# Block inversions with X and XT in the blocks' own tiles, negations on ScalarE, a third result buffer, and v turned one block later

## The chip, the core and the metric

The kernel runs on one core of one Trainium2 chip. The metric is the time of one execution on the device in microseconds (us): the median of three runs before is 1490.18 us (1489.36 to 1492.62). A core has the engines TensorE (PE in the profile, with its weight loads as PEld), VectorE (DVE), ScalarE (ACT), GpSimd (POOL) and SyncE (SP, which here only issues transfers); each runs its own instructions in their order and waits on semaphores for the others. ScalarE and GpSimd issue transfers too.

## The reference, cut to what matters

One layer of a diffusion backbone over 256 context tokens and 1024 latent tokens, so 10 tiles of 128 tokens, with a model width of 1024:

```python
h   = modulated rms_norm of context and latent tokens
p   = h @ w_in                  # q, k, v, z (4 heads of 128), ab, rq, rk, rv, rg
q, k, v = silu(short_conv(q, k, v))     # 5 taps along the tokens
# gated DeltaNet, in chunks of 64 tokens, forward and backward:
A   = tril(kb @ k.T * decay, -1)
sol = solve_triangular(A + I, [v * beta, kb * exp(G)])
S   = gl * S + k_dec.T @ (u - w @ S)    # scan over the chunks
# retention with rotary positions on rq, rk
y   = concat(rms_norm(o_gdn) * silu(z), group_norm(o_ret) * silu(rg))
x   = x + g1 * (y @ w_out)
x   = x + g2 * swiglu(modulated rms_norm(x))
out = rms_norm(x)
```

The change is in the triangular solve (the inverse of `A + I`), in the convolution of v, and in the order of the projections around them.

## The kernel before

The program is written stage by stage, and a scheduler then interleaves the instructions of each engine by its own simulation of the time; so an engine's final order differs from the written one, and a small edit may move many rows. Tiles are taken from pools; a pool that is opened where others were closed takes their room, so its first writer waits for the last readers of what lay there.

Products in full precision are split in a high and a low part: `whi` on ScalarE, `wlo` on VectorE, and three products for each. **Projection columns** come in groups of 256 (`token_major(g, ...)`, its rows are `tm` L371 to L373): one group over the latent tiles is 8 tiles of 24 matmuls, 192 rows. Groups 8 and 9 are z, finished by `fin_gate` on ScalarE; groups 2 to 5 are rk and rq, finished by `fin_rope` on VectorE (L524, L527) and GpSimd (L529), and their result leaves the three `tm` banks of PSUM only by that. **Convolved heads** come from `conv_block` (`b` L605 to L607, 48 to 72 matmuls; taps on VectorE L615; silu on ScalarE L618) into a tile `y`. There are two `y`, one for each of two heads under way.

Around the change the written order is: convolve k, then q; groups 6 and 7; then for batches 0 and 1 (four tiles of tokens each; batch 2 has two) `solve`: for each tile `pre` (`kk` L729, `kq` L734, a broadcast load `gw`, a select on GpSimd, an exponential on ScalarE, and U L748 and `sp` L750 on VectorE), then `invert`; then the four heads of v, each convolved and at once turned by ten transposes (`vT` L871), copied (`vt` L873) and stored; then `pre` of batch 2, `merge(0)`, the load of the rotary table `rope`, `invert(2)`, `merge(1)`, `merge(2)`; then groups 8 and 9, and the scan, with the retention and groups 2 to 5 beside it.

`invert(b)` inverts all 32x32 diagonal blocks of a batch at once, one block a partition. U's blocks are stored to `yd`, loaded again as `yr`, copied or turned into L (L774, L775); X is set to the identity by GpSimd (L771, L772); 31 steps of two VectorE instructions (L781, L783) substitute forward; the turned inverse XT is written to a tile of L's ring (L785); X and XT go to `xd` (L787). X has one buffer and yr one. `merge(b)` then loads the inverses into U and `t64` (L802, L803) and joins blocks to 64 and to 128 by small matmuls on TensorE: products of 32 rows (L822), their negation `xt1` (L825), two more products (L829, L832), copies on ScalarE (L835, L838), and for every eight matrices products of 64 rows (L845), a negation `xt2` (L846), products (L849), a copy (L851). Both negations are on VectorE. U is stored to `sd` (L853), where the scan loads it (`pk`). The pools GM, G2, GI and GU hold the merges' matrices, and are closed behind groups 8 and 9.

Of the kernel before, what the change touches and what calls it, by code (L numbers as in the profile page):

```python
# [8 lines left out]
F32 = mybir.dt.float32  # L9
# [29 lines left out]
def build(nc, tc, ap, dbg=None, stop=None, marks=None):  # L39
# [19 lines left out]
    def close(p):  # L59
        p_close.pop(id(p)).close()  # L60
# [130 lines left out]
    try:  # L191
# [197 lines left out]
        def token_major(g, tiles, finish, store, pl, q=S):  # L389

            w = [tm_weights(g, kh, pl, q) for kh in range(2)]

            for p in range(0, len(tiles), 2):
                pair = [(t, tm_bank(g)) for t in tiles[p:p + 2]]
                for kh in range(2):
                    for t, o in pair:
                        tm_half(o, w[kh], kh, t)
                for t, o in pair:
                    tm_store(g, t, o, finish, store, pl)
# [118 lines left out]

        def fin_rope(t, o, res):
            cos, sin = rope[:, t, 0:64], rope[:, t, 64:128]  # L520
            ra = R1.tile([P, 2, 2, 64], F32, tag="ra", name="ra")
            o4 = o.rearrange("p (h a d) -> p h a d", a=2, d=64)
            r4 = res.rearrange("p (h a d) -> p h a d", a=2, d=64)
            V.tensor_tensor(ra.rearrange("p h a d -> p (h a) d"), o.rearrange("p (g d) -> p g d", d=64),  # L524
                            bc(cos, [P, 4, 64], 1), ALU.mult)
            for a in range(2):
                V.tensor_tensor(r4[:, :, a, :], o4[:, :, 1 - a, :], bc(sin, [P, 2, 64], 1), ALU.mult)  # L527
            for a, op in ((0, ALU.subtract), (1, ALU.add)):
                G.tensor_tensor(r4[:, :, a, :], ra[:, :, a, :], r4[:, :, a, :], op)  # L529
# [88 lines left out]
            S.activation(y[:, a0:], y[:, a0:], AF.Silu)  # L618

        def newy():  # L620
            return CV.tile([P, NTOK], F32, tag="y", name="y", bufs=2)

        a4, b4, kds4, neG4 = (sm[n].rearrange("p (t d h) -> p t d h", d=2, h=4) for n in ("ab", "beta", "kds", "neG"))

# [39 lines left out]
        V.tensor_scalar(sm["g"], sm["neG"], -1.0, None, ALU.mult)  # L664
        V.tensor_scalar(nkf, nkf, EPS, None, ALU.add)

        lnk = log(GS, nkf, TT * H, "ln").rearrange("p (t h) -> p t h", h=H)
        nG4 = sm["nG"].rearrange("p (t d h) -> p t d h", d=2, h=H)
        V.tensor_scalar(lnk, lnk, 0.5, None, ALU.mult)
        Gr = R2.tile([P, TT, 2, H], F32, tag="Gr", name="Gr", bufs=1)  # L670
# [87 lines left out]
        def invert(b):  # L758

            nc_ = len(BATCH[b])  # L760
            nu = nc_ * H
            nb = 4 * nu
            xd = xds[b] = dr.tile([4 * nb, 1024], F32, tag="xd%d" % b, name="xd%d" % b)
            yr = GI.tile([P, 1024], F32, tag="yr", name="yr", bufs=1)
            for k in range(4):
                SY.dma_start(yd[b][:, k].rearrange("u i j -> i u j"),
                             us[b][q32[k]].rearrange("p e c h j -> p (e c h) j")[:, :, q32[k]])
            SY.dma_start(yr[:2 * nb], yd[b].rearrange("u k i j -> (u k) (i j)"))
            L = GI.tile([P, 1024], F32, tag="L", name="L", bufs=2)
            X = GI.tile([P, 1024], F32, tag="X", name="X", bufs=1)  # L770
            G.memset(X, 0.0)  # L771
            G.memset(X[:, 0::33], 1.0)  # L772
            m = lambda t: t[:2 * nb].rearrange("p (i j) -> p i j", j=32)
            S.activation(L[:nb], yr[:nb], AF.Copy)  # L774
            V.tensor_copy(m(L)[nb:], yr[nb:2 * nb].rearrange("p (i j) -> p j i", j=32))  # L775
            for j in range(31):
                n = 31 - j
                tmp = GI.tile([P, 256], F32, tag="tmp", name="tmp", bufs=1)
                t3 = tmp[:2 * nb, :n * (j + 1)].rearrange("p (i c) -> p i c", c=j + 1)
                sh = [2 * nb, n, j + 1]  # L780
                V.tensor_tensor(t3, bc(m(L)[:, j + 1:, j], sh, 2), bc(m(X)[:, j, :j + 1], sh, 1), ALU.mult)  # L781
                xs = m(X)[:, j + 1:, :j + 1]
                V.tensor_tensor(xs, xs, t3, ALU.subtract)  # L783
            XT = GI.tile([P, 1024], F32, tag="L", name="XT", bufs=2)
            V.tensor_copy(m(XT), X[:2 * nb].rearrange("p (i j) -> p j i", j=32))  # L785
            for i, x in enumerate((X[:nb], XT[nb:2 * nb], X[nb:2 * nb], XT[:nb])):
                SY.dma_start(xd[i * nb:(i + 1) * nb], x)  # L787
# [19 lines left out]
        def merge(b):  # L807

            uu, ub, t64 = blocks(b)
            nu = len(BATCH[b]) * H  # L810
            q = q32
            u = [x.rearrange("p c h j -> p (c h) j") for x in ub]
            t = t64


            pairs = [(d, p) + ((2 * p, 2 * p + 1) if d == 0 else (2 * p + 1, 2 * p)) for p in range(2) for d in range(2)]
            three = lambda ps, sl, w: ps[sl].rearrange("p (n j) -> p n j", j=w)
            ps1 = bank_b("m1")
            for n in range(nu):
                for d, p, a, bb in pairs:  # L820
                    ca = (a % 2) * 32
                    T.matmul(ps1[q[bb], n * 32:n * 32 + 32], u[d][q[a], n, q[bb]], t[d][q[a], n, ca:ca + 32],  # L822
                             start=True, stop=True)
            xt1 = GM.tile([P, 16, 32], F32, tag="xt", name="xt1", bufs=1)
            V.tensor_scalar(xt1.rearrange("p n j -> p (n j)")[:, :nu * 32], ps1[:, :nu * 32], -1.0, None, ALU.mult)  # L825
            ps2, ps3 = bank_b("m1"), bank_b("m1")
            for n in range(nu):
                for d, p, a, bb in pairs:
                    T.matmul(ps2[q[a], n * 32:n * 32 + 32], xt1[q[bb], n, :], u[d][q[bb], n, q[bb]],  # L829
                             start=True, stop=True)  # L830
                    if p == d:
                        T.matmul(ps3[q[bb], n * 32:n * 32 + 32], u[d][q[bb], n, q[bb]], xt1[q[bb], n, :],  # L832
                                 start=True, stop=True)
            for d, p, a, bb in pairs:
                S.activation(u[d][q[a], :, q[bb]], three(ps2[:, :nu * 32], q[a], 32), AF.Copy)  # L835
                if p == d:
                    ca = (a % 2) * 32
                    S.activation(t[d][q[bb], :, ca:ca + 32], three(ps3[:, :nu * 32], q[bb], 32), AF.Copy)  # L838
            halves = [(0, slice(0, 64), slice(64, 128)), (1, slice(64, 128), slice(0, 64))]
            for n0 in range(0, nu, 8):  # L840
                ps1, ps2 = bank_b("m2"), bank_b("m2")
                xt2 = GM.tile([P, 8, 64], F32, tag="xt", name="xt2", bufs=1)
                for n in range(8):
                    for d, A, B in halves:
                        T.matmul(ps1[B, n * 64:n * 64 + 64], u[d][A, n0 + n, B], t[d][A, n0 + n, :], start=True, stop=True)  # L845
                V.tensor_scalar(xt2.rearrange("p n j -> p (n j)"), ps1, -1.0, None, ALU.mult)  # L846
                for n in range(8):
                    for d, A, B in halves:
                        T.matmul(ps2[A, n * 64:n * 64 + 64], xt2[B, n, :], u[d][B, n0 + n, B], start=True, stop=True)  # L849
                for d, A, B in halves:  # L850
                    S.activation(u[d][A, n0:n0 + 8, B], three(ps2, A, 64), AF.Copy)  # L851
            for c, t in enumerate(BATCH[b]):
                S.dma_start(sd[t, :, 1:8:6], uu[:, :, c].rearrange("p e h j -> p e (h j)"))  # L853
            checkpoint("mrg%d" % b)

        def solve(b):
            for t in BATCH[b]:
                pre(t)
            checkpoint("pre%d" % b)
            invert(b)  # L860
            checkpoint("inv%d" % b)

        solve(0)
        solve(1)
        for h in range(H):
            y = newy()
            conv_block(8 + h, y, False)
            for t0, n in ((0, 2), (2, 4), (6, 4)):
                ps = bank_a("vT")
                for t in range(t0, t0 + n):  # L870
                    T.transpose(ps[:, (t - t0) * P:(t - t0 + 1) * P], y[:, t * P:(t + 1) * P], ident)  # L871
                vt = CV.tile([P, 4, P], F32, tag="vt", name="vt", bufs=2)
                S.activation(vt[:, :n], ps[:, :n * P].rearrange("p (t j) -> p t j", j=P), AF.Copy)  # L873
                S.dma_start(vd[t0:t0 + n, :, h, :].rearrange("t p j -> p t j"), vt[:, :n])
        close(CV)
        checkpoint("v")
        RP = pool("rp", side="right")
# [13 lines left out]
        merge(2)  # L891


        for g in (8, 9):
            token_major(g, LAT, fin_gate, S, W)
        checkpoint("rgz")
        close(GM)
        close(G2)
# [1 line left out]
        close(GU)  # L900


        SC = pool("sc", bufs=2, side="right")
        PK = pool("pk", side="right")
        dy = dr.tile([LT, P, D], F32, tag="dy", name="dy")
# [247 lines left out]
        close(RT)  # L1153
        close(PK)
        close(SC)
        close(RP)
        close(GS)

# [518 lines left out]
```

## Time and profile before

| what | value |
|---|---|
| median of three runs | 1490.18 us |
| the profiled execution | 1488.32 us |
| its span, first to last instruction | 1486.5 us |
| mean granted TensorE clock | 0.977 |
| busy TensorE / VectorE / ScalarE / GpSimd | 95% / 66% / 42% / 39% of the span |
| TensorE in 360 to 380 us | 11.12 us busy, clock 0.74 |
| TensorE in 520 to 540 us | 20.00 us busy, clock 1.00 |

Sums in the prediction are made against the profiled execution, which was 1.86 us below the median; 1.8 us of it lie outside the span. A row of a view of groups reads: line, engine, operation, what is written and read, how often; busy time and mean of one; the idle time ahead and what ended it. A row of the waits has the sum, how often, and the longest. A row of the timeline has its start, its duration and, in brackets, the wait ahead of it. A row of the windows has the busy time of PE, PEld, DVE, ACT and POOL with the number of instructions, then the granted clock, the share of the DMA engines' time, and GB/s. A row of a list of transfers ends with the time from issue to landing.

### The profile page before, as it was taken

Reading aid. Unit: us, or ns where it says so; the run is one execution under the profiler, and the core shown is the slowest. Engines: PE = TensorE matmul, PEld = TensorE weight load, DVE = VectorE, ACT = ScalarE, POOL = GpSimd, SP = SyncE. Lnnn points to the kernel's source line nnn. Section 1 sums busy time; section 2 is a strip of 40 time slices with the busy share of each in tenths; the row PEclk is TensorE's granted clock in tenths of the full one; section 3 lists DMA queues with packets and bytes.
Section 4 is the critical chain, followed back from the end, with each engine's and each line's share of the span. In section 5 each row is a group of like instructions: output and inputs, shape, how many; then the busy total and the mean of one; then the engine's idle time right before and its main releaser. Section 6 shows DMA issues by size and latency. Waiting matters only on the chain. (4 is left out here: it accounts for less than half of the span.)

```text
span 1486.5 us, 24142 instructions
## 1 busy us (share of the span) xinstructions
PE 1407.3 (95%) x8919; PEld 1207.9 (81%) x8919; DVE 978.0 (66%) x1909; ACT 618.0 (42%) x1342; POOL 579.6 (39%) x493
## 2 busy tenths in 40 slices
PE   7999999996988999899799899999999999999997
PEld 2798888875978999889688688877888888788886
DVE  6568786568666335789777786656555554658577
ACT  5543553866331111346544533323333333444445
POOL 0130010221102344245235588899555553335321
PEclk9999999999889999999899999999999999999999
DMA  9536676478745743996633265765222242685863
GB/s 334 187 105 232 179 235 194 137 221 227 178 130 136 288 165 115 412 367 192 223 124 114 85 210 212 256 236 191 107 107 106 106 145 73 224 293 184 299 220 114
DMA packets 167766, 284.78 MB, mean 192 GB/s; under 512 B 43208, under 2 KB 93592, under 8 KB 163936
## 3 DMA queue, kind: packets, MB, share of 16 engines
q1 hardware_dynamic: 116096, 239.80, 47.6%
q10 hardware_dynamic: 49072, 35.83, 7.8%
q0 software_dynamic: 2480, 7.60, 1.4%
q8 instruction: 70, 1.15, 0.3%
q14 instruction: 48, 0.39, 0.1%
HBM read 201.36 MB, written 81.84 MB: 191 GB/s over the span
## 5 line engine op out<-in xcount | busy, mean ns | idle before, releaser
L371 PE MATMUL tm<-whi,hhi 128*128 128x256 f32 (+1 forms) x704 | 202.7, 293 | 7.5 <-ACT whi L344 3.0
L372 PE MATMUL tm<-wlo,hhi 128*128 128x256 f32 (+1 forms) x704 | 202.8, 290 | 0.7 <-DVE wlo L345 0.7
L373 PE MATMUL tm<-whi,hlo 128*128 128x256 f32 (+1 forms) x704 | 201.4, 290 | 0.0
L371 PEld LDWEIGHTS tm<-whi,hhi 128*128 128x128 f32 x704 | 136.0, 195 | 10.7 <-ACT whi L344 3.2
L372 PEld LDWEIGHTS tm<-wlo,hhi 128*128 128x128 f32 x704 | 137.2, 195 | 2.7 <-DVE wlo L345 1.2
L1366 PE MATMUL ffn<-t,wlo 128*128 128x512 f32 x352 | 137.1, 390 | 1.6 <-DVE wlo L345 1.6
L1364 PE MATMUL ffn<-t,whi 128*128 128x512 f32 x352 | 137.0, 390 | 1.4 <-ACT whi L344 1.4
L373 PEld LDWEIGHTS tm<-whi,hlo 128*128 128x128 f32 x704 | 136.3, 195 | 1.6 <-issue 0.9
L1365 PE MATMUL ffn<-t,whi 128*128 128x512 f32 x352 | 137.0, 389 | 0.0
L344 ACT ACTIVATE whi<-wraw 128x512 fp32r<-128x512 f32 (+2 forms) x98 | 75.2, 771 | 133.1 <-PE ffn L1365 80.2
L344 ACT ACTIVATE whi<-ws 128x512 fp32r<-128x512 f32 x88 | 55.6, 632 | 173.8 <-PE ffn L1365 121.0
L345 DVE TENSOR_TENSOR wlo<-ws,whi 128x512 fp32r<-128x512 f32 x88 | 94.7, 1078 | 48.4 <-ACT whi L344 48.2
L1490 PE MATMUL fo<-whi,ahi 128*128 128x512 f32 x308 | 119.3, 389 | 1.0 <-ACT ahi L344 1.0
L1491 PE MATMUL fo<-wlo,ahi 128*128 128x512 f32 x308 | 119.9, 389 | 0.0
L1492 PE MATMUL fo<-whi,alo 128*128 128x512 f32 x308 | 119.0, 390 | 0.0
L345 DVE TENSOR_TENSOR wlo<-wraw,whi 128x512 fp32r<-128x512 f32 (+2 forms) x92 | 101.5, 1105 | 19.5 <-ACT whi L344 19.2
L1364 PE MATMUL ffn<-b,whi 128*128 128x512 f32 x264 | 103.9, 394 | 5.1 <-ACT whi L344 5.1
L1366 PE MATMUL ffn<-b,wlo 128*128 128x512 f32 x264 | 103.6, 392 | 0.7 <-DVE wlo L345 0.7
L1365 PE MATMUL ffn<-b,whi 128*128 128x512 f32 x264 | 103.4, 392 | 0.0
L615 DVE SCALAR_TENSOR_TENSOR y<-u,cw,y 128x1022 f32<-128x1022 f32 (+3 forms) x80 | 81.9, 1040 | 19.7 <-ACT y L609 19.2
L607 PE MATMUL b<-hhi,wlo 128*128 128x512 f32 (+1 forms) x256 | 94.7, 370 | 0.0
L606 PE MATMUL b<-hlo,whi 128*128 128x512 f32 (+1 forms) x256 | 94.3, 368 | 0.0
(451 smaller groups left out, 3440.1 us busy)
## 6 DMA issues: line engine op xcount, KB each, us to landing
adaw<-ada SPq DMA_DIRECT2D x48, 512.0 KB, 4.4
pk<-sd SPq DMA_DIRECT2D x16, 1536.0 KB, 15.0
wraw<-wfi SPq DMA_DIRECT2D x44, 512.0 KB, 4.2
ar<-ad SPq DMA_DIRECT2D x33, 512.0 KB, 4.2
w<-wfo SPq DMA_DIRECT2D x22, 512.0 KB, 4.3
wd<-tw SPq DMA_DIRECT2D x11, 1024.0 KB, 4.9
ad<-act SPq DMA_DIRECT2D x20, 512.0 KB, 3.1
raw<-wd SPq DMA_DIRECT2D x20, 512.0 KB, 4.7
```

The costliest lines, as they stand in the source:

```text
L344: S.activation(hi, raw, AF.Copy)
L345: e.tensor_tensor(lo, raw, hi.bitcast(F32), ALU.subtract)
L371: T.matmul(o, hhi[:, k, tsl], whi[:, k % 4, :], start=(k == 0), stop=False)
L372: T.matmul(o, hhi[:, k, tsl], wlo[:, k % 4, :], start=False, stop=False)
L373: T.matmul(o, hlo[:, k, tsl], whi[:, k % 4, :], start=False, stop=(k == KT - 1))
L607: T.matmul(o, wlo[:, k, :], hh, start=False, stop=(k == KT - 1))
L1364: T.matmul(o, whi[:, k, :], xhi(xn, slice(0, 4), k), start=(first and k == 0), stop=False, **kw)
L1365: T.matmul(o, whi[:, k, :], xlo(xn, slice(0, 4), k), start=False, stop=False, **kw)
L1366: T.matmul(o, wlo[:, k, :], xhi(xn, slice(0, 4), k), start=False, stop=(k == 3), **kw)
L1490: T.matmul(po[g][i], ahi[:, ts], whi, start=(j == 0 and not kw), stop=False, **kw)
L1491: T.matmul(po[g][i], ahi[:, ts], wlo, start=False, stop=False, **kw)
L1492: T.matmul(po[g][i], alo[:, ts], whi, start=False, stop=(j == FH - 1), **kw)
```

## The change

Four things, in the diff below:

- **invert**: `yr` is gone. The upper rows of the reloaded blocks go straight to X, the lower ones to L, in two loads; L's turned half is copied from X, and then VectorE sets X to the identity. XT is written into L itself. X has two buffers.
- **merge**: both negations are ScalarE copies with a scale of -1.
- **v**: the y tiles are three; head h is turned behind the convolution of head h+1, and head 3 behind group 8, which is written ahead of it now. The copies `vt` hold two transposes each, so there are five stores a head in place of three.
- **room**: the rope stage's temporary `ra` has a pool of its own, RA, opened behind the merges' pools and ahead of the scan's; the temporary of one logarithm moves from the pool GS to R2.

```diff
@@ fin_rope
-            ra = R1.tile([P, 2, 2, 64], F32, tag="ra", name="ra")
+            ra = RA.tile([P, 2, 2, 64], F32, tag="ra", name="ra")
@@ newy
-            return CV.tile([P, NTOK], F32, tag="y", name="y", bufs=2)
+            return CV.tile([P, NTOK], F32, tag="y", name="y", bufs=3)
@@
-        lnk = log(GS, nkf, TT * H, "ln").rearrange("p (t h) -> p t h", h=H)
+        lnk = log(R2, nkf, TT * H, "ln").rearrange("p (t h) -> p t h", h=H)
@@ invert
-            yr = GI.tile([P, 1024], F32, tag="yr", name="yr", bufs=1)
+            L = GI.tile([P, 1024], F32, tag="L", name="L", bufs=2)
+            X = GI.tile([P, 1024], F32, tag="X", name="X", bufs=2)
...
-            SY.dma_start(yr[:2 * nb], yd[b].rearrange("u k i j -> (u k) (i j)"))
-            L = GI.tile([P, 1024], F32, tag="L", name="L", bufs=2)
-            X = GI.tile([P, 1024], F32, tag="X", name="X", bufs=1)
-            G.memset(X, 0.0)
-            G.memset(X[:, 0::33], 1.0)
+            rows = yd[b].rearrange("u k i j -> (u k) (i j)")
+            SY.dma_start(X[nb:2 * nb], rows[nb:])
+            SY.dma_start(L[:nb], rows[:nb])
             m = lambda t: t[:2 * nb].rearrange("p (i j) -> p i j", j=32)
-            S.activation(L[:nb], yr[:nb], AF.Copy)
-            V.tensor_copy(m(L)[nb:], yr[nb:2 * nb].rearrange("p (i j) -> p j i", j=32))
+            V.tensor_copy(m(L)[nb:], X[nb:2 * nb].rearrange("p (i j) -> p j i", j=32))
+            V.memset(X, 0.0)
+            V.memset(X[:, 0::33], 1.0)
...
-            XT = GI.tile([P, 1024], F32, tag="L", name="XT", bufs=2)
+            XT = L
             V.tensor_copy(m(XT), X[:2 * nb].rearrange("p (i j) -> p j i", j=32))
@@ merge
-            V.tensor_scalar(xt1.rearrange("p n j -> p (n j)")[:, :nu * 32], ps1[:, :nu * 32], -1.0, None, ALU.mult)
+            S.activation(xt1.rearrange("p n j -> p (n j)")[:, :nu * 32], ps1[:, :nu * 32], AF.Copy, scale=-1.0)
...
-                V.tensor_scalar(xt2.rearrange("p n j -> p (n j)"), ps1, -1.0, None, ALU.mult)
+                S.activation(xt2.rearrange("p n j -> p (n j)"), ps1, AF.Copy, scale=-1.0)
@@ v
+        def vturn(h, y):
             for t0, n in ((0, 2), (2, 4), (6, 4)):
                 ps = bank_a("vT")
                 for t in range(t0, t0 + n):
                     T.transpose(ps[:, (t - t0) * P:(t - t0 + 1) * P], y[:, t * P:(t + 1) * P], ident)
-                vt = CV.tile([P, 4, P], F32, tag="vt", name="vt", bufs=2)
-                S.activation(vt[:, :n], ps[:, :n * P].rearrange("p (t j) -> p t j", j=P), AF.Copy)
-                S.dma_start(vd[t0:t0 + n, :, h, :].rearrange("t p j -> p t j"), vt[:, :n])
+                for t in range(t0, t0 + n, 2):
+                    vt = CV.tile([P, 2, P], F32, tag="vt", name="vt", bufs=2)
+                    S.activation(vt, ps[:, (t - t0) * P:(t - t0 + 2) * P].rearrange("p (t j) -> p t j", j=P), AF.Copy)
+                    S.dma_start(vd[t:t + 2, :, h, :].rearrange("t p j -> p t j"), vt)
...
+        vys = []
         for h in range(H):
-            y = newy()
-            conv_block(8 + h, y, False)
+            vys.append(newy())
+            conv_block(8 + h, vys[h], False)
+            if h:
+                vturn(h - 1, vys[h - 1])
+        token_major(8, LAT, fin_gate, S, W)
+        vturn(H - 1, vys[H - 1])
         close(CV)
...
-        for g in (8, 9):
-            token_major(g, LAT, fin_gate, S, W)
+        token_major(9, LAT, fin_gate, S, W)
...
+        RA = pool("ra", bufs=2, side="right")
         SC = pool("sc", bufs=2, side="right")
```

The scheduler's order moves with it. TensorE, end of the v part, before (numbers behind a name count tiles; `y_3774` is head 2, `y_3894` head 3, `tm_4895` the first tile of group 8):

```order
L607 MATMUL b2_3956<-hhi_86,wlo_3896 128x512
L734 MATMUL kq_4032<-qc_4030,kc_4023 128x128 x4
L729 MATMUL kk_4065<-kc_4063 128x128 x4
L871 MATMUL vT_3872<-ident_65,y_3774 128x128 x2
L871 MATMUL vT_3878<-ident_65,y_3774 128x128 x4
L871 MATMUL vT_3886<-ident_65,y_3774 128x128 x4
L734 MATMUL kq_4072<-qc_4070,kc_4063 128x128 x4
L871 MATMUL vT_3992<-ident_65,y_3894 128x128 x2
L871 MATMUL vT_3998<-ident_65,y_3894 128x128 x4
L871 MATMUL vT_4006<-ident_65,y_3894 128x128 x4
L371 MATMUL tm_4895<-whi_4883,hhi_86 128x256
```

The same place now, from the last convolution's end to group 8's first row (`y_3754` is head 2):

```order
L607 MATMUL b2_3942<-hhi_86,wlo_3882 128x512
L729 MATMUL kk_4281<-kc_4279 128x128 x2
L734 MATMUL kq_4288<-qc_4286,kc_4279 128x128 x3
L868 MATMUL vT_3978<-ident_65,y_3754 128x128 x2
L868 MATMUL vT_3984<-ident_65,y_3754 128x128 x4
L868 MATMUL vT_3995<-ident_65,y_3754 128x128 x4
L734 MATMUL kq_4288<-qc_4286,kc_4279 128x128
L729 MATMUL kk_4321<-kc_4319 128x128 x4
L371 MATMUL tm_4018<-whi_4006,hhi_86 128x256
```

Head 3's transposes and the last kq have moved behind group 8's 192 rows, ahead of group 9 (`y_3880` is head 3, `tm_4187` group 8's last tile, `tm_5149` group 9's first):

```order
L373 MATMUL tm_4187<-whi_4012,hlo_87 128x256
L868 MATMUL vT_4242<-ident_65,y_3880 128x128 x2
L734 MATMUL kq_4328<-qc_4326,kc_4319 128x128 x4
L868 MATMUL vT_4248<-ident_65,y_3880 128x128 x4
L868 MATMUL vT_4259<-ident_65,y_3880 128x128 x4
L371 MATMUL tm_5149<-whi_5137,hhi_86 128x256
```

TensorE, end of merge 2 before (`U2` and `t64_4742` are batch 2; `tm_5736`, `tm_5813` and those behind are tiles of groups 2 and 3):

```order
L373 MATMUL tm_5736<-whi_5465,hlo_87 128x256
L845 MATMUL m2_4843<-t64_4742,U2_4022 64x64 x15
L371 MATMUL tm_5813<-whi_5801,hhi_86 128x256
L371 MATMUL tm_5814<-whi_5801,hhi_86 128x256
L372 MATMUL tm_5813<-wlo_5802,hhi_86 128x256
...
L373 MATMUL tm_5813<-whi_5807,hlo_87 128x256
L849 MATMUL m2_4844<-U2_4022,xt2_4845 64x64 x16
L948 MATMUL Tr_5372<-pk0_5367 128x128 x4
```

And now, from merge 1's last products to the scan's first transposes (`U1` is batch 1; `tm_5559` is the fourth tile of group 2):

```order
L849 MATMUL m2_4955<-U1_3015,xt2_4956 64x64 x16
L822 MATMUL m1_5006<-t64_4996,U2_4278 32x32 x32
L829 MATMUL m1_5041<-U2_4278,xt1_5039 32x32
L832 MATMUL m1_5042<-xt1_5039,U2_4278 32x32
...
L845 MATMUL m2_5097<-t64_4996,U2_4278 64x64 x16
L849 MATMUL m2_5098<-U2_4278,xt2_5099 64x64 x16
L957 MATMUL Tr_5393<-pk0_5388 128x128 x4
L957 MATMUL Tr_5400<-pk1_5391 128x128 x4
L964 MATMUL up_5407<-vn_5398,pk0_5388 128x128 x4
L371 MATMUL tm_5559<-whi_5480,hhi_86 128x256
```

Before, 276 rows of groups 2 and 3 stood among the merges, the last ones between merge 2's stages; now 72 rows (three tiles of group 2) stand ahead of merge 1's last products, and none from there to behind merge 2 and the scan's first products.

VectorE, where invert 1 ends and invert 2 begins, now (`L_3421` holds XT of batch 1, `X_4627` and `L_4626` are batch 2, `wlo_5481` is group 2's first low part):

```order
L783 TENSOR_TENSOR X_3422<-X_3422,tmp_3522 128x31
L785 COPY L_3421<-X_3422 128x1024
L781 TENSOR_TENSOR tmp_4637<-L_4626,X_4627 64x31
...
L783 TENSOR_TENSOR X_4627<-X_4627,tmp_4652 64x26x6
L345 TENSOR_TENSOR wlo_5481<-wraw_5482,whi_5480 128x4x256
L781 TENSOR_TENSOR tmp_4655<-L_4626,X_4627 64x175
...
L785 COPY L_4626<-X_4627 64x1024
L524 TENSOR_TENSOR ra_5543<-tm_5492,rope_4274 128x256
```

The first low part of group 2 stands behind invert 1 as before, and the first rope stage, which stood in the middle of invert 2, stands behind its end. The copy of batch 2's L, which needs the blocks stored and loaded again, stands ahead of invert 1's last eight steps.

More of the change, by code (lines that the diff above doesn't have):

```diff
@@ L861, in solve @@
             checkpoint("inv%d" % b)
-        solve(0)
-        solve(1)
-        for h in range(H):
-            y = newy()
-            conv_block(8 + h, y, False)
+        def vturn(h, y):
             for t0, n in ((0, 2), (2, 4), (6, 4)):
@@ L871, in build @@
                     T.transpose(ps[:, (t - t0) * P:(t - t0 + 1) * P], y[:, t * P:(t + 1) * P], ident)
-                vt = CV.tile([P, 4, P], F32, tag="vt", name="vt", bufs=2)
-                S.activation(vt[:, :n], ps[:, :n * P].rearrange("p (t j) -> p t j", j=P), AF.Copy)
-                S.dma_start(vd[t0:t0 + n, :, h, :].rearrange("t p j -> p t j"), vt[:, :n])
+                for t in range(t0, t0 + n, 2):
+                    vt = CV.tile([P, 2, P], F32, tag="vt", name="vt", bufs=2)
+                    S.activation(vt, ps[:, (t - t0) * P:(t - t0 + 2) * P].rearrange("p (t j) -> p t j", j=P), AF.Copy)
+                    S.dma_start(vd[t:t + 2, :, h, :].rearrange("t p j -> p t j"), vt)
+        solve(0)
+        solve(1)
+        vys = []
+        for h in range(H):
+            vys.append(newy())
[4 more added lines that the diff above has]
+        vturn(H - 1, vys[H - 1])
         close(CV)
@@ L1155, in build @@
         close(SC)
+        close(RA)
         close(RP)
```

## The prediction

> **What bounds the kernel now.** I read the page first, then the waits of TensorE between 300 and 510 us, then the same stretch cut into windows.
>
> ```profile
> PE 1407.3 (95%) x8919; PEld 1207.9 (81%) x8919; DVE 978.0 (66%) x1909; ACT 618.0 (42%) x1342; POOL 579.6 (39%) x493
> ```
>
> TensorE works 95% of the span, so an edit on another engine pays only where TensorE waits for it or runs at a lowered clock. The edits act where v is convolved and turned (until 373 us) and on groups 8, 9, 2, 3 with the three merges (373 to 500 us). The waits there:
>
> ```profile
> PE vT L871 <- ACT y L618: 11.2, 3, 8.7
> PE kq L734 <- issue: 5.2, 2, 2.6
> PE m L822 <- DMA t<-xd: 4.8, 4, 2.3
> PE tm L371 <- ACT whi L344: 3.0, 1, 3.0
> PE m L829 <- issue: 2.6, 1, 2.6
> ```
>
> So 16.4 us of waits lie in the v part (vT and kq), and 10.4 in the merges. Pauses also cost clock:
>
> ```profile
> 360.00:380.00 20.00, 11.12 (x72) 10.93 (x73) 17.87 (x34) 10.52 (x18) 2.44 (x2) 0.74 0.56 166
> 400.00:420.00 20.00, 16.94 (x397) 16.11 (x398) 16.70 (x41) 5.50 (x10) 0.00 (x0) 0.77 0.43 106
> 440.00:460.00 20.00, 17.90 (x258) 16.78 (x263) 13.97 (x35) 2.55 (x4) 5.10 (x9) 0.83 0.69 181
> ```
>
> The column behind POOL's is the granted clock: 0.74, 0.77 and 0.83 of full. What that does to a row of the projection:
>
> ```profile
> 401.13 0.41 PE L371 MATMUL tm<-whi,hhi 128*128 128x256 f32 x1
> 401.35 0.41 PE L372 MATMUL tm<-wlo,hhi 128*128 128x256 f32 x1
> ...
> 500.84 0.28 PE L373 MATMUL tm<-whi,hlo 128*128 128x256 f32 x1
> 500.96 0.28 PE L371 MATMUL tm<-whi,hhi 128*128 128x256 f32 x1
> ```
>
> Start to start, a row takes 0.12 us at full clock and 0.21 at the lowered one: 0.09 lost for each slow row.
>
> **The v part.** The last head's v is turned right behind its own convolution:
>
> ```profile
> 360.15 1.31 PE L871 MATMUL vT<-ident,y 128*128 128x128 f32 x10 [1.35 <-ACT y L618]
> ...
> 371.08 2.40 PE L871 MATMUL vT<-ident,y 128*128 128x128 f32 x10 [8.73 <-ACT y L618]
> 373.13 0.56 PE L371 MATMUL tm<-whi,hhi 128*128 128x256 f32 x1
> ```
>
> Before 371.08 TensorE has nothing but vT and waits 8.73 us for taps and silu of y; with the third y each head is turned a block later, and head 3 behind all of group 8. Group 8 began at 373.1. Less 16.4 of waits, less 1.1 of slow vT (2.40 against 1.31), less 2.2 for head 3's vT (1.31) and the last kq (about 0.9), which now stand behind group 8, that is 353.4 if nothing new waits. Something will: VectorE, which frees the banks of kk and kq and makes y, was itself busy 17.9 of 20 us in 360 to 380. The order has five places where kq, vT or a convolution needs a bank or a y early. Bounds: none of it, or the old 16.4. The nearest rows are the kq waits of 2.6; I take five of 1 to 2, **7 us** in all, and 1 us of clock. Group 8 begins at **361.4**, 11.7 earlier.
>
> The vt tiles of two transposes cost ACT and its queue two more copies and stores a head. ACT worked 10.5 of 20 us there, so I put this at nothing; uncovered it would be eight copies, under 0.4 us each. The log's temporary costs nothing: same rows, another pool.
>
> **The inversions.** XT in L's place and loads straight into X and L remove the ScalarE copy; the memsets go to VectorE.
>
> ```profile
> DVE xt L825 <- PE m L822: 6.9, 2, 4.9
> DVE xt L846 <- PE m L845: 5.7, 2, 4.2
> DVE tmp L781 <- POOL X L772: 7.6, 2, 5.1
> ```
>
> VectorE stood 12.6 us in merges 0 to 2 before negations, and 7.6 behind GpSimd's memset, which waited for the single X to be stored. Both go. VectorE gains three memsets of 1024. No row shows one there; the bounds are nothing, where VectorE would have waited anyway, and its copy of 1024 elements, 1.13 below; I take 1.0 each, near the copy, plus 0.2 for the diagonal. [...]
>
> The negations go to ScalarE at about 0.6 us, taken from its copies of 512 elements from the same banks (two in 1.19, below). Nothing else needs ScalarE in those stages.
>
> **The path that sets the end of the stretch.** In the new order the rope stage of group 2 (ra) can't start before merge 2's matrices are stored, since ra's pool takes the merges' room. So 72 rows of group 2 fill the three banks, and TensorE then runs the rest of merges 1 and 2 with no projection between. I follow this chain on the clock of the run before.
>
> TensorE: group 8's 192 rows at 0.12 take 23.0 (384.4), vT and kq 2.2 (386.6), 119 rows of group 9 14.3 (400.9), then 76 rows 9.1 with merge 0's two product stages and one of its four 64-row stages. Those I put at 4.5; their busy time in the rows below, 2/5 of three sums and 1/5 of one, is 7.3, an upper bound since rows overlap. At **414.5** it stands at group 2's first row with wlo, the low part of the weights.
>
> ```profile
> L845 PE MATMUL m<-t,U 64*64 64x64 f32 x160 | 6.6, 221 | 0.0
> ...
> L822 PE MATMUL m<-t,U 32*32 32x32 f32 x320 | 5.1, 194 | 4.9 <-DMA t<-xd 4.8
> L829 PE MATMUL m<-U,xt 32*32 32x32 f32 x320 | 5.0, 202 | 2.6 <-issue 2.6
> L832 PE MATMUL m<-xt,U 32*32 32x32 f32 x160 | 4.9, 203 | 0.0
> ```
>
> VectorE: this wlo stands behind invert 1's end, which stands behind invert 2's L copy, its load, the yd store, and the last U of batch 2; the exponential for that U stands on ScalarE behind the 96th row of group 9 (398.1). From there: res 0.4, table load and exponential 1.28 each, U 0.7, store 1.2 and 3.7, loads 1.2 and 4.1, L copy 1.1, memset 1.2, eight rows of invert 1 2.0, XT 1.1, twelve short rows of invert 2 3.1, wlo 1.2: 22.3 more, so 420.4. With 2.5 for queueing (SP also issues merge 0's loads between) **423**. TensorE waits 8.5.
>
> ```profile
> 383.74 1.28 ACT L745 ACTIVATE gw<-gw,nG 128x128 f32<-128x128 f32 x4
> 385.05 1.28 ACT L532 ACT_TABLE_LOAD   x1
> ...
> gw<-grow_d SPq DMA_DIRECT2D x13, 256.0 KB, 4.9
> ...
> yr<-yd SPq DMA_DIRECT2D x2, 512.0 KB, 4.1
> ...
> yd<-U SPq DMA_DIRECT2D x4, 64.0 KB, 3.7
> ```
>
> Head 3's vT closes the convolutions' pool, and rope's load takes that room; on SP's queue gw for that U and half of merge 0's t stand behind it. vT ends at 386.6; with its copy and the wait for its store (about 3) and gw's 4.9 they land near 395 to 397. That is before 398.1 and 400.9, so I add nothing; if it takes 5 more, the chain behind moves with it.
>
> Then invert 2: 62 rows took 21.7 in all (11.1 and 10.6 below), the twelve done 3.1; with a second wlo the end is 19.8 later, 442.8.
>
> ```profile
> L783 DVE TENSOR_TENSOR X<-X,tmp 64x31 f32<-64x31 f32 (+15 forms) x31 | 11.1, 358 | 0.9
> L781 DVE TENSOR_TENSOR tmp<-L,X 64x31 f32<-64x31 f32 (+15 forms) x31 | 10.6, 342 | 3.3 <-POOL X L772 2.5
> ```
>
> From XT to the first full run of merge 2's products took 12.3 before (469.40 to 481.68); in batch 1 21.6 (XT at 428.44, last issue ended 446.65, landing 3.4).
>
> ```profile
> 388.15 1.13 DVE L785 COPY XT<-X 128x1024 f32<-128x1024 f32 x1
> ...
> 428.44 1.06 DVE L785 COPY XT<-X 128x1024 f32<-128x1024 f32 x1
> ...
> 469.40 1.05 DVE L785 COPY XT<-X 64x1024 f32<-64x1024 f32 x1
> ...
> 440.79 5.86 SPq L803 DMA_DIRECT2D t<-xd  x4
> ...
> 481.68 0.70 PE L822 MATMUL m<-t,U 32*32 32x32 f32 x58 [0.73 <-DMA t<-xd]
> ...
> 498.82 1.19 ACT L851 ACTIVATE U<-m 64x512 f32<-64x512 f32 x2 [5.54 <-PE m L849]
> ...
> sd<-U ACTq DMA_DIRECT2D x10, 512.0 KB, 5.6
> ```
>
> I take 12.3, as this is the same batch: merge 2 starts at **455**. Bare, it costs products 0.9 and 1.0, copies 2.2, two 64-row stages of about 1.1, two negations 0.4 and 0.6, some 7.7 with the hand-overs, and 1 for the lowered clock; the copies of U 1.2, the store 0.9 and 5.6, ra and res 0.9: group 2's next row starts at **472**.
>
> By then 456 projection rows are done (192 + 192 + 72). Before, they were these when the scan's first transposes ended, at 500.5:
>
> ```profile
> L371 PE MATMUL tm<-whi,hhi 128*128 128x256 f32 x221 | 66.4, 308 | 4.5 <-ACT whi L344 3.0 <-DVE res L527 1.4
> L372 PE MATMUL tm<-wlo,hhi 128*128 128x256 f32 x220 | 66.2, 303 | 0.3 <-DVE wlo L345 0.3
> L373 PE MATMUL tm<-whi,hlo 128*128 128x256 f32 x219 | 65.9, 303 | 0.0
> ```
>
> That is 660. The transposes are done in the pause now. The other 204 cost 24.5 at 0.12 and 2.4 for some 27 slow rows after the pause: 499. So of the 11.7 us earned, about 10 go back to bare merges, and 1.5 to 2 stay, with 0.5 for the up product that is also done. Behind this point the order on TensorE is nearly the old one.
>
> [...]
>
> **Sum.** The profiled execution took 1488.32 us, 1.86 below the median of the runs (1490.18). 1488.3 less 2.2 is 1486.1; on the median's footing **1488.0**.
>
> **Rivals.** (a) *Shorter stalls, 11 us more gained.* If wlo isn't held by the late U (the exponential passes group 9's results sooner), invert 1 ends by its own work: XT 0 some 9 us earlier than its 388.15, and from XT 0 to XT 1 the old 40.3 less 5.1 for the memset and some 6 for negations and ra: 408 instead of 418. All behind moves by as much: 1477. For it: VectorE sheds 20 us of waits. Against: the chain above, all in a fixed order. (b) *Slower.* Merge 2's transfers take batch 1's 21.6, not 12.3, beside merge 1's stores and the scan's loads: +9.3, net +7: 1495; it decides once merge 2's data come more than 3 us later than 455. For: windows of that stretch show the DMA at 0.43 to 0.69 busy, and the loads now follow closer on the stores. Against: batch 2 is half the size. (c) *The v part isn't shortened*, since VectorE, 17.9 of 20 busy, holds kq and vT as it did: the dates of both chains move 10 to 11 later, and the bare merges remain: 1497. (d) *The merges stay filled*: the forecast's 10 us of giving back don't occur at all; that is (a) by another way.
>
> **Chances.** Forecast 0.47, with a range of its own of 1484 to 1492 (the 7 us of new waits may be 4 or 11, the queueing 0 or 5); (a) and (d) 0.24; (b) 0.21; (c) 0.08. What a measurement can tell from no change here is 0.2%, 3 us. Of the forecast, 0.17 lies below 1487.2 and 0.02 above 1493.2: faster 0.41, same 0.28, slower 0.31. The range runs from (a) to just over (c): **1477 to 1498**.
>
> **What would show it.** Group 8's first row near 361; a wait of TensorE of 6 to 10 us on group 2's wlo near 415; merges 1 and 2 with no projection row inside, and a wait for the loads of t before merge 2; projection rows resuming at 470 to 475. Rival (a) shows as no wait on wlo; (b) as merge 2's first product after 460; (c) as group 8 at 370 or later. Wrong altogether would be a change behind 500 us: I give the scan, the output projection and the FFN nothing.

## The result, and the profile after

The change made the kernel slower. In runs beside one another it took 1497.32 us (1496.62 to 1498.59, 4 runs), the kernel before 1489.77 us (1487.52 to 1492.62, 4 runs): ratio 1.0051, 95% interval 1.0031 to 1.007, so about 7.6 us. The profiled execution took 1496.62 us, 8.3 more than the one before (1488.32). I had forecast 1488.0, a little faster or the same; the time lies inside my range, on its far side. Slow executions are left out of the medians and ratios below: one of e6 (1986.5 us) and two of the kernel before.

The waits of TensorE between 300 and 510 us, after the change, largest first (waiter, what ended the wait, sum, times, longest):

```profile
PE m L845 <- ACT t L838: 5.2, 4, 2.0
PE kS L939 <- DVE S L967: 4.4, 1, 4.4
PE m L822 <- DMA t<-xd: 4.1, 3, 3.4
PE m L829 <- issue: 3.5, 2, 2.5
PE tm L372 <- DVE wlo L345: 3.4, 2, 3.2
PE m L849 <- ACT xt L846: 2.6, 3, 1.2
PE tm L371 <- ACT vt L871: 2.2, 2, 1.1
PE m L829 <- ACT xt L825: 2.0, 1, 2.0
```

The waits of vT on y (11.2) and most of kq's (5.2, now 2.1) are gone. In their place stand waits inside the merges: their products for ScalarE's copies and negations, each between two stages of one merge. The same stretch in windows, after (PE first; behind POOL the granted clock):

```profile
360.00:380.00 20.00, 18.79 (x144) 17.73 (x143) 19.38 (x40) 10.03 (x17) 1.81 (x1) 1.00 0.35 111
400.00:420.00 20.00, 18.31 (x424) 17.22 (x423) 10.01 (x24) 6.77 (x13) 2.39 (x2) 1.00 0.70 155
440.00:460.00 20.00, 11.94 (x405) 10.97 (x405) 11.70 (x33) 5.33 (x10) 0.00 (x0) 0.80 0.66 178
460.00:480.00 20.00, 13.43 (x344) 12.32 (x343) 1.60 (x8) 7.88 (x16) 0.84 (x3) 0.67 0.78 265
```

At 360 to 380 TensorE works 18.79 us instead of 11.12, at full clock. At 440 to 460 it works 11.94 where it had 17.90, and from 460 to 480 it works 13.43 at a clock of 0.67, where before it was:

```profile
460.00:480.00 20.00, 16.99 (x407) 15.87 (x393) 13.20 (x40) 5.79 (x10) 5.85 (x12) 1.00 0.48 127
```

What it does in those 40 us stands in the groups of instructions cut to 440 to 480 us. The projection's three groups before:

```profile
L371 PE MATMUL tm<-whi,hhi 128*128 128x256 f32 x62 | 18.9, 314 | 4.5 <-ACT whi L344 3.0 <-DVE res L527 1.4
L372 PE MATMUL tm<-wlo,hhi 128*128 128x256 f32 x62 | 18.6, 303 | 0.3 <-DVE wlo L345 0.3
L373 PE MATMUL tm<-whi,hlo 128*128 128x256 f32 x61 | 18.2, 301 | 0.0
```

And after the change:

```profile
L372 PE MATMUL tm<-wlo,hhi 128*128 128x256 f32 x11 | 3.9, 357 | 0.0
L373 PE MATMUL tm<-whi,hlo 128*128 128x256 f32 x11 | 3.7, 340 | 0.0
L371 PE MATMUL tm<-whi,hhi 128*128 128x256 f32 x9 | 3.1, 347 | 0.0
```

185 rows against 31: 154 rows fewer, 18.5 us at 0.12 each. That shows that the projection has left the merges, but it isn't the loss, for in the same 40 us the change does 704 of the merges' small matmuls and the kernel before 452: merge 2 ends at 478.3 in the change and at 498.8 before. Counted at the same place of the program, the kernel before has 660 rows done at 500.5, behind the scan's first transposes; the change has 456 done at 483.0, behind these and the first up product (0.8 us). The 204 missing rows are 24.5 us, so there the change is **some 6 us behind** (507.5 against 501.3), although it began group 8 6.7 us ahead. So 13 us went in between; 1.9 of them are head 3's turn and the last kq, which now stand behind group 8. VectorE shows what holds the rows (its waits from 430 to 500 us, after):

```profile
DVE ra L524 <- PE m L849: 25.6, 1, 25.6
```

The first rope stage of group 2 waits 25.6 us for merge 2's last product. The dates of the chain that I had followed, after the change (each row is cut to a short window, so its count is not the whole group):

```profile
366.44 0.38 PE L371 MATMUL tm<-whi,hhi 128*128 128x256 f32 x1
...
446.85 1.38 PE L822 MATMUL m<-t,U 32*32 32x32 f32 x86 [3.42 <-DMA t<-xd]
...
467.60 0.59 PE L822 MATMUL m<-t,U 32*32 32x32 f32 x46
...
478.23 0.58 PE L957 MATMUL Tr<-pk 128*128 128x128 f32 x1
...
483.04 0.36 PE L371 MATMUL tm<-whi,hhi 128*128 128x256 f32 x1
...
493.17 0.58 PE L939 MATMUL kS<-S,pk 128*128 128x128 f32 x1 [4.44 <-DVE S L967]
```

Group 8 starts at 366.4 (before 373.1). Merge 1's products start at 446.9 and merge 2's at 467.6, with nothing to wait for between them but the merge itself; 17 rows stand behind merge 1's first products, and none from 452.4 on. The projection goes on at 483.0.

### The profile page after: what moved, and what is told of

Same layout as the page of the kernel before. It is cut to its first block, busy times and chain, and to the rows that moved or that the text cites. A ratio compares the mean times of both kernels' runs of the same rounds, so it can differ in the third digit from the quotient of the medians.

```text
span 1494.6 us, 24154 instructions
## 1 busy us (share of the span) xinstructions
PE 1402.7 (94%) x8919; PEld 1205.8 (81%) x8919; DVE 971.3 (65%) x1907; ACT 622.4 (42%) x1355; POOL 575.2 (38%) x487
## 4 chain that ended last, share of the span: by engine, by line
PE 50%; DMA 10%; DVE 8%; POOL 6%; ACT 3%; issue 3%; SPq 0%; ACTq 0%; POOLq 0%; DVEq 0%
PE ffn L1376 6%; PE ffn L1374 6%; PE ffn L1375 6%; PE fo L1502 4%; PE fo L1500 4%; PE fo L1501 4%; PE tm L373 3%; PE tm L371 3%; PE tm L372 3%; DMA wd<-tw 2%; PE op L1235 2%; PE op L1234 2%; PE op L1233 2%; DMA t<-xd 1%; POOL ws L1347 1%
## 5 line engine op out<-in xcount | busy, mean ns | idle before, releaser
L371 PE MATMUL tm<-whi,hhi 128*128 128x256 f32 (+1 forms) x704 | 199.3, 288 | 6.0 <-ACT vt L871 2.2
L605 PE MATMUL b<-hhi,whi 128*128 128x512 f32 (+1 forms) x256 | 94.6, 370 | 1.3 <-ACT y L609 1.3
```

Source lines behind the costliest of these rows:

```text
L371: T.matmul(o, hhi[:, k, tsl], whi[:, k % 4, :], start=(k == 0), stop=False)
```

## The experiments

All ran beside the kernel before, which had a median of 1488.9 to 1489.7 us in these runs; e1 to e4 ran on one chip, e5 to e11 on another, so between these the ratios compare better than the medians. Ratios are to it, with 95% intervals; the changed kernel's is 1.0051. The last column counts projection rows between the first and the last matmul of the merges, from the profile of each.

| run | edit | median us | ratio (interval) | rows |
|---|---|---|---|---|
| before | | 1489.77 | 1 | 468 |
| change | | 1497.32 | 1.0051 (1.0031 to 1.007) | 145 |
| e1 | change, ra's pool early | 1484.16 | 0.9965 (0.9952 to 0.9979) | 354 |
| e2 | change, third y only for v | 1506.25 | 1.0112 (1.0098 to 1.0125) | 109 |
| e3 | e1 and e2 together | 1483.06 | 0.9959 (0.9943 to 0.9975) | 352 |
| e4 | change, negations on VectorE | 1502.53 | 1.008 (1.0062 to 1.0098) | 145 |
| e5 | change, head 3 turned inside group 8 | 1502.88 | 1.0105 (1.0083 to 1.0127) | 225 |
| e6 | e1, v turned at once | 1490.35 | 1.0016 (1.0 to 1.0033) | 326 |
| e7 | e1, negations on VectorE | 1485.18 | 0.9976 (0.9959 to 0.9993) | 330 |
| e8 | e1, inversion as before | 1487.66 | 0.999 (0.9976 to 1.0003) | 400 |
| e9 | before, ra's pool late | 1506.44 | 1.012 (1.0093 to 1.0147) | 264 |
| e10 | before, negations on ScalarE | 1482.55 | 0.995 (0.9933 to 0.9968) | 512 |
| e11 | e3, head 3 turned inside group 8 | 1486.78 | 0.9978 (0.9964 to 0.9993) | 403 |

### e1 and e9: the room of ra

e1 takes the changed kernel and opens ra's pool ahead of the merges' pools:

```diff
+        RA = pool("ra", bufs=2, side="right")
         GM = pool("gm", side="right")
...
-        RA = pool("ra", bufs=2, side="right")
         SC = pool("sc", bufs=2, side="right")
```

> Only the pool of the rope temporary is opened ahead of the merges' pools, so it no longer takes their room; all else is the changed kernel. Theory A (the room of ra keeps groups 2 and 3 out of the merges, and the bare merges cost some 19 us against before): projection rows of groups 2 and 3 stand between the stages of merges 1 and 2 again, the q part is unchanged with its wait of about 5 us on qt, and the time falls by 8 to 19 us from 1497, to 1478 to 1489. Rival B (the late chain from the last gw load over invert 1 and invert 2 to the merges' loads sets the pace, whoever owns the room): the waits move to wlo and to the loads of t, and the time stays within 4 us of 1497.

1484.16 us, 13 below the change: theory A held. Rival B fell by the time, though TensorE's wait for merge 1's loads did grow (6.74 us here, 3.42 in the change). In the groups of e1 from 440 to 480 us 148 projection rows are back (31 in the change; this profiled execution took 1489.0 us, 4.8 above e1's median):

```profile
L372 PE MATMUL tm<-wlo,hhi 128*128 128x256 f32 x50 | 15.6, 312 | 0.0
L371 PE MATMUL tm<-whi,hhi 128*128 128x256 f32 x49 | 15.1, 308 | 0.0
L373 PE MATMUL tm<-whi,hlo 128*128 128x256 f32 x49 | 14.9, 304 | 0.0
```

e9 makes the reverse test, that edit alone on the kernel before:

```diff
-            ra = R1.tile([P, 2, 2, 64], F32, tag="ra", name="ra")
+            ra = RA.tile([P, 2, 2, 64], F32, tag="ra", name="ra")
...
+        RA = pool("ra", bufs=2, side="right")
         SC = pool("sc", bufs=2, side="right")
```

> The kernel before with one edit: ra comes from a pool opened behind the merges' pools, as in the change. Theory A (this room alone empties the merges and costs 13 to 19 us net): merges 1 and 2 run with no projection row, and the time is 1502 to 1509. Rival (the loss needs the change's other edits, the late last U and the later turn among them): 1490 to 1498.

1506.44 us: theory A again. This one edit costs 1.2% on the kernel before, 17 to 18 us; the rest of the change together gained 9 to 10. Merge 1's products begin at 455.0 us in e9, as in the kernel before (454.9), and the first row behind the merges comes at 491.7, with 456 rows done. In the change these two dates are 446.9 and 483.0, 8 to 9 us earlier: by these dates, what the other edits gain with bare merges is the earlier start of merge 1. Windows of e9 show the same picture as the change:

```profile
440.00:460.00 20.00, 14.26 (x343) 13.19 (x343) 13.70 (x31) 2.55 (x4) 0.00 (x0) 0.91 0.70 165
460.00:480.00 20.00, 11.92 (x337) 10.47 (x337) 8.14 (x23) 5.78 (x10) 0.00 (x0) 0.55 0.62 162
480.00:500.00 20.00, 14.12 (x135) 13.23 (x135) 4.11 (x15) 4.41 (x10) 4.44 (x9) 0.76 0.98 368
```

TensorE works 11.92 of 20 us at 460 to 480, at a clock of 0.55.

### e2 and e3: the third result buffer

After the change TensorE loses time in the q part too (qt are transposes of q that ScalarE squares and sums): it works 38.80 us of the 45 from 255 to 300, where it had 44.96. Its longest wait there:

```profile
PE qt L686 <- ACT qt L688: 5.4, 1, 5.4
```

With a third y the scheduler had drawn the last q convolution forward; ScalarE then had exponentials, silu, squares and copies mixed, and loaded its tables six times from 265 to 290 us (three times before), 1.28 us each. e2 gives the third buffer to head 2 of v alone, so that k and q have two again:

```diff
-            return CV.tile([P, NTOK], F32, tag="y", name="y", bufs=3)
+            return CV.tile([P, NTOK], F32, tag="y", name="y", bufs=2)
...
-            vys.append(newy())
+            vys.append(CV.tile([P, NTOK], F32, tag="y3", name="y3", bufs=1) if h == 2 else newy())
```

> The third result buffer serves head 2 of v alone; k and q have two again, as before; all else is the changed kernel. Theory A (the third buffer lets the scheduler draw the last q convolutions forward, ScalarE then alternates between exponential, silu and square, and TensorE waits for qt: 9.4 us lost by 293 us): the wait of 5.4 us on qt is gone, and the time falls by 6 to 11 us from 1497, to 1486 to 1491. Rival C (the early part's loss is hidden, since VectorE's inversions set the dates of the merges): the wait goes, but the time stays within 3 us of 1497.

A miss, for theory and rival. The wait on qt went, but the time rose to 1506.25 us. The waits of e2 from 300 to 370 us show where the gain went first:

```profile
PE kq L734 <- issue: 6.2, 2, 4.9
PE tm L371 <- ACT vt L871: 3.1, 1, 3.1
```

Group 8 starts at 364.8 in e2, and at 366.4 in the change: what the q part no longer loses, the v part does, ahead of kq (6.2 us, put down to issue) and for vt (3.1). So the q part's loss is real, and most of it is paid again in the v part; rival C had it hidden too, but by another way and without the rise. The further 9 us are lost behind group 8, with 109 rows under the merges. e3 adds e1's edit:

> Both edits at once: ra's pool opened early, and the third result buffer for head 2 of v alone. Theory A: the two costs lie in different stretches and add: 1470 to 1481, 10 to 18 us below the kernel before (1489.8). Rival: one hides the other, and the time is that of the better single edit, 1484 to 1488.

1483.06 us: near the rival's range and 1 us below it, 2 above the theory's. With the merges filled, the third buffer's place makes no difference that these intervals show (0.9959 against 0.9965 for e1).

### e4, e7 and e10: the negations

e4 and e7 put them back on VectorE, e10 moves them to ScalarE in the kernel before:

```diff
-            V.tensor_scalar(xt1.rearrange("p n j -> p (n j)")[:, :nu * 32], ps1[:, :nu * 32], -1.0, None, ALU.mult)
+            S.activation(xt1.rearrange("p n j -> p (n j)")[:, :nu * 32], ps1[:, :nu * 32], AF.Copy, scale=-1.0)
...
-                V.tensor_scalar(xt2.rearrange("p n j -> p (n j)"), ps1, -1.0, None, ALU.mult)
+                S.activation(xt2.rearrange("p n j -> p (n j)"), ps1, AF.Copy, scale=-1.0)
```

> The changed kernel with both negations of the merges on VectorE again. TensorE's order is nearly the same. My theory: the place of the negations is worth little, within 3 us of 1497 either way, since in the bare merges a negation is on the path on either engine (0.60 us on ScalarE, 0.69 on VectorE). Rival: with the negations behind ScalarE's copies the bare merges are longer, and VectorE, free after invert 2, makes them 4 us or more shorter: below 1493. Other rival: VectorE's wait for the products delays invert 2, and the time is 1501 or more.

> The kernel with ra's pool opened early (1484), and the merges' negations on VectorE again. Theory: with projection rows between the stages a negation is covered on either engine, but VectorE's waits for the products delay the inversion of batch 2 by several us, and so the loads of merge 2: 1485 to 1489. Rival: covered altogether, within 2 us of 1484.

> The kernel before with one edit: both negations of the merges on ScalarE. Theory: VectorE loses 12.6 us of waits for products, invert 2 ends earlier, and TensorE's waits for merge 2's loads shrink by 1 to 4 us: 1485 to 1489. Rival: no change, within 1.5 us of 1489.5.

On VectorE they cost the change some 5 us (1502.53, intervals that just overlap), which is the second rival: XT of batch 2 comes at 456.2 instead of 451.7. In the filled merges of e1 they cost 1 us (1485.18), which the intervals don't separate and which fits theory and rival alike. On the kernel before the move gains 7 us (1482.55), more than I expected. XT of batch 1, which began at 428.44 before, in the timeline of e10:

```profile
419.16 1.07 DVE L785 COPY XT<-X 128x1024 f32<-128x1024 f32 x1
```

VectorE ends invert 1 nine us earlier; its waits before the products (12.6 us before) are gone. The merges end at nearly the same date (499.2 against 498.8), but 512 projection rows lie under them, 44 more than before, 5.3 us at 0.12. The profiled execution took 1485.25 us, 2.7 above the median, and the FFN's first product comes 2.8 us earlier in it than before (836.1 against 838.8), so this profile shows only part of the gain. Alone the move is as fast as e3; of the parts, only this one and ra's room were run alone.

### e5 and e11: the late chain

In the change the rotary table's load waits for head 3's stores on SP's queue (8.7 us, until 402.35), and the last gw load stands behind it (402.80). e5 turns head 3 behind four tiles of group 8:

```diff
-        token_major(8, LAT, fin_gate, S, W)
-        vturn(H - 1, vys[H - 1])
+        w8 = [tm_weights(8, kh, W) for kh in range(2)]
+        for p in range(0, len(LAT), 2):
...
+            if p == 2:
+                vturn(H - 1, vys[H - 1])
```

> The changed kernel with head 3 turned in the middle of group 8, behind four of its eight tiles, with the weights loaded once as before; so the rotary table's load and the last gw load come some 11 us earlier. ra's room is as in the changed kernel. Theory A1 (part of what the merges cost is the late chain: head 3's stores, rope, gw, the last U, the inversions of batches 1 and 2): the wait on wlo goes, merges 1 and 2 get their data 5 to 10 us earlier, and the time falls by 5 to 10 us from 1497, to 1487 to 1492. Rival (the bare merges alone set the loss): within 3 us of 1497.

> The fastest kernel so far (ra's pool early, the third result buffer for head 2 of v alone, 1483) with head 3 turned in the middle of group 8. With filled merges the earlier rope and gw loads bring the loads of merges 1 and 2 forward: 1476 to 1482. Rival: as in the run on the changed kernel, the earlier turn brings nothing or loses some: 1483 to 1488.

In e5 theory and rival fell. The last U came 11 us earlier in e5 (399.6 against 410.6), but XT of batch 2 came at 455.6 instead of 451.7, because VectorE stood 7.07 us behind ScalarE's high part of group 2 in the middle of invert 2:

```profile
443.06 1.23 DVE L345 TENSOR_TENSOR wlo<-wraw,whi 128x1024 fp32r<-128x1024 f32 x1 [7.07 <-ACT whi L344]
```

So the data came 1.3 us earlier to merge 1 (445.5 against 446.9) and not to merge 2, the merges ended nearly where they had (477.6 against 478.3), and the time was 6 to 8 us worse than the change's (by medians and by ratios). With filled merges (e11) the rival held: 1486.78 us, no better than e3's 1483.06. An earlier turn brings nothing there. What an earlier date of both inversions is worth to bare merges e5 doesn't show, since it didn't move the second.

### e6 and e8: the later turn, and the inversion

e6 turns each head at once in e1's kernel (first diff); e8 has the old inversion in it (second diff):

```diff
-            if h:
-                vturn(h - 1, vys[h - 1])
+            vturn(h, vys[h])
         token_major(8, LAT, fin_gate, S, W)
-        vturn(H - 1, vys[H - 1])
```

```diff
-            SY.dma_start(X[nb:2 * nb], rows[nb:])
-            SY.dma_start(L[:nb], rows[:nb])
+            SY.dma_start(yr[:2 * nb], yd[b].rearrange("u k i j -> (u k) (i j)"))
...
-            V.memset(X, 0.0)
+            G.memset(X, 0.0)
...
-            XT = L
+            XT = GI.tile([P, 1024], F32, tag="L", name="XT", bufs=2)
```

> The kernel with ra's pool opened early (1484), and each head of v turned at once again behind its own convolution, head 3 ahead of group 8, in the new narrow tiles. Theory: the later turn is what takes the waits on y away, and it is worth 5 to 10 us: a wait of about 8 us on y returns before group 8, and the time is 1489 to 1494. Rival (VectorE sets the dates of the stretch, and the waits on vT are paid elsewhere without it): 1481 to 1487.

> The kernel with ra's pool opened early (1484), and the inversion as before: one load into a tile of its own, one X, GpSimd's memsets, ScalarE's copy, XT in a tile of L's ring. Theory: VectorE waits 5 to 8 us again for the memsets behind X's store, XT of batches 1 and 2 are that much later, and TensorE waits 3 to 8 us more in the merges: 1487 to 1492. Rival: the projection rows cover it: within 2 us of 1484.

e6 took 1490.35 us, 6 to 8 above e1 (by medians and by ratios): it lies in the theory's range, and with filled merges the later turn is worth that. The wait before the last vT returns, here put down to VectorE (timeline of e6):

```profile
377.26 2.40 PE L868 MATMUL vT<-ident,y 128*128 128x128 f32 x10 [7.24 <-DVE X L783]
```

Group 8 begins at 379.3 in e6 and at 365.5 in e1, so of 13.8 us there about half reaches the end.

e8 took 1487.66 us, 3.5 above e1, with intervals that just overlap. VectorE's waits for GpSimd's memset are back in it, 9.5 us:

```profile
DVE tmp L781 <- POOL X L772: 9.5, 2, 5.7
```

## Why the prediction was wrong

**The mechanism was right.** I had named it: ra's pool takes the merges' room, 72 rows of group 2 fill the banks, and merges 1 and 2 run bare. e1 and e9 show it from both sides. **Its size was wrong**, and with that the sign. By my sum the v part earned 11.7 us and the bare merges took about 10 back. Measured, ra's room costs 13 us in the change (e1) and 17 to 18 in the kernel before (e9), and group 8 began 6.7 us earlier.

**The term that failed** is "merge 2 starts at 455". Its products began at 467.6, 12.6 later, and the rows went on at 483.0 and not 472. Two steps ahead of it were wrong.

The first had no term. I took the path to run over VectorE to merge 2's loads, and priced only merge 2 as bare. Merge 1 was all but bare as well, and stood on TensorE ahead of merge 2: its products began at 446.9, when its own loads had landed, and it took until 467.6, 20.7 us with 17 rows in them. Merge 2's last load was issued at 460.3, some 9 us behind XT (451.7), and TensorE shows no wait for it. By my own dates merge 1 would have started at 439.6 (XT of batch 1 at 418, as in rival (a), and the 21.6 of that batch; measured 21.1) and ended at 460.3: about 5 of the 12.6.

The rest is lateness of the chain on VectorE, from a term that I put at nothing. I let rope's and gw's loads land at 395 to 397 and wrote "so I add nothing; if it takes 5 more, the chain behind moves with it". After the change:

```profile
396.84 0.38 ACT L871 ACTIVATE vt<-vT 128x256 f32<-128x256 f32 x1 [3.69 <-DMA sd<-vt]
...
400.03 0.39 ACT L871 ACTIVATE vt<-vT 128x256 f32<-128x256 f32 x1 [1.64 <-DMA sd<-vt]
...
402.35 0.35 SPq L896 DMA_DIRECT2D rope<-rope  x1
402.80 0.38 SPq L737 DMA_DIRECT2D gw<-grow_d  x1
...
407.91 1.28 ACT L745 ACT_TABLE_LOAD   x1 [1.45 <-DMA gw<-grow_d]
...
410.58 0.69 DVE L748 TENSOR_TENSOR U<-kk,gw 128x512 f32<-128x512 f32 x1 [5.50 <-ACT gw L745]
...
420.99 1.05 DVE L773 COPY L<-X 32x1024 f32<-32x1024 f32 x1 [4.91 <-DMA X<-yd]
...
425.79 1.11 DVE L785 COPY L<-X 128x1024 f32<-128x1024 f32 x1
```

Head 3's vT ended at 393.2 (386.6 in my sum, as group 8 had begun 5 us late and TensorE had waited for vt once), and from there to rope's load it took 9.2 us, where I had about 3: five stores went through two vt tiles, and ScalarE's copies waited 3.69, 0.50 and 1.64 us for them. So gw landed at 407.9, some 11 behind my 397; wlo was done at 431.4 (423), XT of batch 1 began at 425.8 (418) and XT of batch 2 at 451.7 (442.8). I had priced the two more copies and stores a head by ScalarE's busy time, at nothing; what counted was the wait for the stores. That this moved the end is read from the dates; no run took it away alone. In the kernel before, the way from head 3's vT to rope's load took 4.4 us (373.5 to 377.9), with three stores and one wait of 0.82 us for them, so the narrower tiles go with 4.8 of the 9.2 us. (My list of steps from 398.1 to wlo also adds up to 23.6, not 22.3, a slip of 1.3.)

A bare merge is a chain of stages that hand over between TensorE and ScalarE, at a lowered clock (0.80 and 0.67); merge 2 too took 10.7 us (467.6 to 478.3) and not 8.7.

**The store was not a term.** I let ra wait for U's copies and store, 1.2, 0.9 and 5.6. It started at merge 2's last product; the first copy of U ran beside it. The scan's first transposes and up products, on a slow clock (0.50 from 478 to 482 us), took that time instead, 4.8 us from merge 2's end to the next row where I had 8.6. So this error was 4 us in the other direction. The 2.4 for some 27 slow rows behind the pause was an estimate that no run shows: from 483.24 on the rows already came 0.12 us apart. Between a few rows the scan's first steps then stood bare as well (kS, the product of the keys with the state S, waited 4.44 us).

**The v part.** I put group 8 at 361.4; it came at 366.4. The 7 us for new waits weren't the reason: those shown from 300 to 370 us are under 2 us each and 5 in all. It began late, by the wait on qt in the q part, to which I gave nothing. e2 and e3 show that taking it away moves this start little: without that wait group 8 comes at 364.8 and 364.7. The turn itself is worth 6 to 8 us at the end (e6), not 11.7; the wait on y went as forecast.

**What held.** Memsets and the in-place XT pay, by 3.5 us (e8, at the edge of the intervals). A wait on wlo came, with 3.3 us and not 8.5: wlo was 8.4 late, and TensorE came 13.7 late to that row (428.2 for 414.5). Behind the scan nothing changed: the FFN's first product stands at 847.5 and stood at 838.8, 8.7 us later, and the span is 8.1 us longer.

**The rivals.** (b) had the direction and nearly the time (1495), and its mark, merge 2's first product after 460, came too; but it gave slow transfers as the reason, and TensorE waited for none of batch 2's. (c) had 1497, the measured time, by chance: its mark was group 8 at 370 or later, and it was 366.

What stays open: why e2 and e5 lose another 6 to 9 us against the change where their merges are bare. Rows under the merges are 109 and 225, and e5 has more than the change. Both show a long wait of the scan's kS on S (8.1 and 10.5 us, 4.4 in the change), and the copy of S ahead of it waited 9.66 and 10.73 us (3.80 in the change), put down to the stores of the merges' U. The 3.7 and 6.0 us more on kS would be part of e2's loss and most of e5's, but no run took that wait away by itself.

## What to carry to other kernels

A tile that is given "free" room in a pool opened later inherits the last readers of what lay there (ra's first writer waited 25.6 us here); ask what its first writer then holds up, and who waits behind that one. When a stage loses its covering work, price the whole chain of hand-overs of every piece that lost it, not the last piece alone. Compare the work done at the same place of the program, not in the same stretch of time: the stretch said 18.5 us here, and taking the cause away gave 13. Price a transfer through few buffers by its stores, not by its copies (here a copy took 0.35 to 0.39 us and waited up to 3.69 for a store). And test the parts alone: one line of this change alone cost 17 to 18 us, the negations alone gained 7, and both were hidden in one verdict of 0.5%.

## What was not expected of the hardware

VectorE's memset of 128x1024 took 0.91 us and the diagonal's 0.09 (timeline of the change), a little under the 1.0 and 0.2 of the sum, of which the 1.0 was put near a copy of 1.13 and the 0.2 stood on no row:

```profile
358.03 0.91 DVE L774 MEMSET X<- 128x1024 f32 x1 [0.16 <-DVE y L615]
...
360.79 0.09 DVE L775 MEMSET X<- 128x32 f32 x1
```

On the clock: it fell inside merge 1 with no pause over 2 us. From 453.7 to 459.0 us TensorE did small matmuls, 1.03 us of work, with pauses of 1.02, 1.28 and 1.96 us, and the granted clock went from 1.00 to 0.50:

```profile
456.00:458.00 2.00, 0.32 (x2) 0.19 (x2) 0.00 (x0) 1.95 (x5) 0.00 (x0) 1.00 0.30 55
458.00:460.00 2.00, 1.03 (x20) 1.03 (x22) 0.00 (x0) 0.91 (x2) 0.00 (x0) 0.70 0.61 99
460.00:462.00 2.00, 1.25 (x22) 1.07 (x22) 0.00 (x0) 0.60 (x1) 0.00 (x0) 0.50 0.82 131
```

So the fall follows a stretch in which TensorE worked about 1 of 5 us in short pieces; which part of it brought the fall, no run shows.
